# SwiGLU over 8192 rows: four-row groups with all transfers on one DMA queue, in place of two-row tiles with loads and stores on separate queues

## The chip, the cores and the metric

The kernel runs on one core of a Trainium2 chip. The metric is device time in microseconds, the median of the runs. "The span" is the time from the first to the last instruction in one execution that the hardware profiler recorded; all views of the profile are of that execution.

The core has engines that work side by side and wait for each other through semaphores: ScalarE (ACT) applies functions, VectorE (DVE) multiplies, SyncE (SP) and GpSimd (POOL) here only start transfers. A transfer (DMA) between the chip's main memory (HBM) and the on-chip memory (SBUF, 128 partitions) is started by an instruction on SP, ACT or POOL. Each of the three has a queue of its own. The data are moved by 16 DMA engines, which serve all queues.

## The reference

```python
x = np.random.randn(8192, 8192).astype(np.float32)
a, b = np.split(x, 2, axis=-1)
silu_b = b / (1 + np.exp(-b))
return a * silu_b
```

A row of x has 8192 numbers: the first 4096 are a, the last 4096 are b. The output row has 4096. So 268.44 MB are read and 134.22 MB written, and each output needs one function value and one product.

## The kernel before, in words

A tile takes two rows (R = 2) on each of the 128 partitions: 65536 B per partition, 8 MiB, one solid block of x. There are 32 tiles. Three slots in SBUF of that size (`slot0` to `slot2`) are used in turn; together they take 192 KiB of each partition. For each tile:

- `load` (L54, the DMA at L55) is a DMA on SP's queue: x to the slot.
- `swiglu` (L67): ACT applies Silu to b in place (L72), then DVE multiplies a and b and writes the product into the first half of the same slot (L76). The product needs half the room: 32768 B per partition.
- `store` (L81, the DMA at L85) writes that half to the output, 4 MiB. It is issued from ACT's queue; five stores in the middle of the kernel are issued from POOL's, and the stores of the last two tiles from SP's.

Between them the waits are: the gate waits for the load, the product for the gate, the store for the product, and the load of tile i + 3 for the store of tile i, which empties its slot. The order on each engine is written out by hand in the loop at L93, with `manual_schedule`; `declare_no_dep` takes out the waits that follow from others. On SP, the loads stand in the order of the tiles; a load that waits holds back all behind it.

The beginning and the end are cut finer. Tiles 0 to 2 are computed row by row (128x4096). The store of tile 0 is in three pieces (4096, 12288 and 16384 B per partition), and its slot is refilled by two half loads, the second half (32768 B of each 65536 B) as soon as the second row's product is done. The last tile (31) is loaded in two halves and stored in three pieces, the last products being 128x2048.

Of the kernel before, what the change touches and what calls it, by code (L numbers as in the profile page):

```python
# [1 line left out]

# [4 lines left out]

_SILU = mybir.ActivationFunctionType.Silu


@with_exitstack
def kernel(
    ctx: ExitStack,
    tc: tile.TileContext,
    x: bass.AP,
    out: bass.AP,
):

    nc = tc.nc
    N, M = x.shape
    half = M // 2
    P = nc.NUM_PARTITIONS
    R = 2
    BUFS = 3  # L30

    xv = x.tensor.reshape([N // R, R * M]).ap()
    ov = out.tensor.reshape([N // R, R * half]).ap()
    ntiles = N // (P * R)
    last = ntiles - 1

    pool = ctx.enter_context(tc.tile_pool(name="sbuf", bufs=1))
    ctx.enter_context(tc.manual_schedule())
    slots = [pool.tile([P, R * M], x.dtype, name=f"slot{s}") for s in range(BUFS)]
    loads, gates, prods, stores = ([[] for _ in range(ntiles)] for _ in range(4))  # L40

    newest = {}

    def follows_from_others(inst, i, current, earlier):


        targets = [t for kind in current for t in kind[i]]
        targets += [t for kind in earlier for j in range(i % BUFS, i, BUFS) for t in kind[j]]
        for t in targets:
            if t is not newest.get(inst.ins.engine):  # L50
                tc.declare_no_dep(inst.ins, t.ins, reason="ordered by the other waits")
        newest[inst.ins.engine] = inst

    def load(i, c0=0, cw=R * M, free=None):  # L54
        inst = nc.sync.dma_start(  # L55
            out=slots[i % BUFS][:, c0 : c0 + cw], in_=xv[i * P : (i + 1) * P, c0 : c0 + cw]
        )
        if free:
            for t in loads[i - BUFS] + gates[i - BUFS] + prods[i - BUFS] + stores[i - BUFS]:
                if t is not free and t is not newest.get(inst.ins.engine):  # L60
                    tc.declare_no_dep(inst.ins, t.ins, reason="ordered by the other waits")
            newest[inst.ins.engine] = inst
        else:
            follows_from_others(inst, i, [], [loads, gates, prods])
        loads[i].append(inst)

    def swiglu(i, k0=0, k1=R, c0=0, cw=half, gated=None):  # L67
        rows = slots[i % BUFS].rearrange("p (k s c) -> p k s c", k=R, s=2)
        a = rows[:, k0:k1, 0, c0 : c0 + cw]
        b = rows[:, k0:k1, 1, c0 : c0 + cw]  # L70
        o = slots[i % BUFS][:, : R * half].rearrange("p (k c) -> p k c", k=R)
        gate = nc.scalar.activation(out=b, in_=b, func=_SILU)  # L72
        follows_from_others(gate, i, [], [loads, gates, prods, stores])
        if gated:
            gated()
        prod = nc.vector.tensor_mul(out=o[:, k0:k1, c0 : c0 + cw], in0=a, in1=b)  # L76
        follows_from_others(prod, i, [loads], [loads, gates, prods, stores])
        gates[i].append(gate)
        prods[i].append(prod)

    def store(i, c0=0, cw=R * half):  # L81
        eng = nc.scalar if i < last - 1 else nc.sync
        if i % 2 and ntiles // 2 <= i < ntiles // 2 + 10:
            eng = nc.gpsimd
        inst = eng.dma_start(  # L85
            out=ov[i * P : (i + 1) * P, c0 : c0 + cw], in_=slots[i % BUFS][:, c0 : c0 + cw]
        )
        follows_from_others(inst, i, [loads, gates], [loads, gates, prods, stores])
        stores[i].append(inst)

    for i in range(BUFS):
        load(i)
    for i in range(last):  # L93
        if i == 0:

            swiglu(i, 0, 1)
            swiglu(i, 1, 2, gated=lambda: [store(0, 0, half // 4), store(0, half // 4, half * 3 // 4)])
            load(BUFS, M, M, free=prods[0][-1])
            store(i, half, half)
        elif i < BUFS:  # L100
            for k in range(R):
                swiglu(i, k, k + 1)
            store(i)
        else:
            swiglu(i)
            if i == last - 1:
                swiglu(last, 0, 1)
            store(i)
        nxt = i + BUFS
        if nxt == BUFS:  # L110
            load(nxt, 0, M)
        elif nxt < last:
            load(nxt)
        elif nxt == last:
            load(last, 0, M)
            load(last, M, M)

    store(last, 0, half)
    for c0 in range(0, half, half // 2):
        swiglu(last, 1, 2, c0, half // 2)  # L120
    store(last, half, half)


# [1 line left out]
_INS = ['x']  # L125
_OUTS = [((8192, 4096), 'float32')]


# [23 lines left out]
```

## Time and profile before

| | |
|---|---|
| median of 3 runs | 935.29 us (934.9 to 935.36) |
| span of the profiled execution | 934.1 us; no other time of that execution is given |
| VectorE busy | 278.9 us, 30% |
| ScalarE busy | 226.8 us, 24% |
| mean rate of the transfers | 431 GB/s |
| gate (ACT), 128x8192 / 128x4096 | 7029 / 3609 ns |
| product (DVE), 128x8192 / 128x4096 | 8693 / 4425 ns |
| load, 8 MiB, from issue to landing | 37.1 us (median of 30) |
| store, 4 MiB, from ACT's queue | 34.7 us (median of 24) |

How to read the profile: in the row of forty slices, each digit is the busy share of one fortieth of the span in tenths, for the DMA row the mean of the 16 engines. A row of the windows gives, for a stretch of time, its length, the busy time and the number of instructions of each engine, the clock, the share of the DMA engines' time that was filled, and the rate. A packet is counted in the window in which it starts, so short windows can show shares above 1. A row of the timeline gives the start, the length and the engine, and in brackets how long the engine had been idle and what ended that.

Under these views lie the single packet records of the trace: for each packet its queue, start, duration and size. Each DMA of 128 partitions is split over 16 engines, 8 packets on each, and each engine ends its share with a write of 4 B to the semaphore.

### The profile page before, as it was taken

What the parts mean: (1) busy time and instruction counts of PE and PEld (TensorE: products, weight loads), DVE (VectorE), ACT (ScalarE), POOL (GpSimd) and SP (SyncE); (2) the same over time, 40 slices, a digit from 0 to 9 for tenths busy, and PEclk for the clock granted to TensorE, in tenths of its full rate; (3) what the DMA queues carried; (4) which work ended last, traced back from release to release, by engine and by line L of the source; (5) the groups of instructions that cost most, each with busy time, mean ns of one, the idle gap of its engine ahead of it and who ended that gap; (6) DMA issues with size and microseconds to landing.
All of it is one profiled execution on the core that took longest, in us unless ns stands there. A gap on an engine that the chain in (4) does not pass through costs nothing.

```text
span 934.1 us, 228 instructions
## 1 busy us (share of the span) xinstructions
DVE 278.9 (30%) x37; ACT 226.8 (24%) x38; POOL 3.0 (0%) x9
## 2 busy tenths in 40 slices
DVE  0333123332133321333312333133331233312342
ACT  0431320233302333113331133311333113331141
POOL 0000000000000000000000000000000000000000
DMA  9999999999999999999999999999999999999998
GB/s 404 418 425 435 429 450 424 446 429 425 448 420 436 427 450 425 425 439 452 432 415 455 413 443 428 431 445 427 431 428 459 415 428 445 429 445 428 428 427 383
DMA packets 9937, 402.67 MB, mean 431 GB/s; under 512 B 1104, under 2 KB 1104, under 8 KB 1232
## 3 DMA queue, kind: packets, MB, share of 16 engines
q1 hardware_dynamic: 5328, 276.83, 68.6%
q10 hardware_dynamic: 3888, 104.86, 26.0%
q0 software_dynamic: 720, 20.97, 5.2%
q14 instruction: 1, 0.01, 0.0%
HBM read 268.44 MB, written 134.22 MB: 431 GB/s over the span
## 4 chain that ended last, share of the span: by engine, by line
DMA 74%; DVE 10%; ACT 7%; issue 6%; another core or an unknown queue 1%; DVEq 0%; SPq 0%; POOL 0%; ACTq 0%; POOLq 0%
DMA slot<-in_x_dram 40%; DMA out_dram<-slot 34%; DVE slot L76 10%; ACT slot L72 7%; DVEq L147 0%; SPq L55 0%; POOL out_dram L85 0%; ACTq L85 0%; DVEq L76 0%; POOLq L147 0%
## 5 line engine op out<-in xcount | busy, mean ns | idle before, releaser
L76 DVE TENSOR_TENSOR slot<-slot 128x8192 f32<-128x8192 f32 (+2 forms) x37 | 278.9, 7539 | 641.4 <-ACT slot L72 641.1
L72 ACT ACTIVATE slot<-slot 128x8192 f32<-128x8192 f32 (+2 forms) x37 | 225.5, 6105 | 690.0 <-DMA slot<-in_x_dram 690.0
L85 POOL DMA_DIRECT2D out_dram<-slot x5 | 2.8, 558 | 756.8 <-DVE slot L76 756.8
L72 ACT ACT_TABLE_LOAD x1 | 1.3, 1283 | 0.7 <-PEq L136 0.7
L136 POOL MEMSET const-bfloat16-1.0<- 128x1 bf16 x1 | 0.1, 102 | 0.0
L136 POOL MEMSET const-float32-0.0<- 128x1 f32 x1 | 0.1, 98 | 0.2 <-issue 0.2
L136 POOL MEMSET const-float32-1.0<- 128x1 f32 x1 | 0.1, 98 | 0.0
L136 POOL MEMSET const-uint8-127<- 128x1 uint8 x1 | 0.1, 98 | 0.0
## 6 DMA issues: line engine op xcount, KB each, us to landing
out_dram<-slot ACTq DMA_DIRECT2D x24, 4096.0 KB, 34.7
out_dram<-slot POOLq DMA_DIRECT2D x5, 4096.0 KB, 33.8
slot<-in_x_dram SPq DMA_DIRECT2D x4, 4096.0 KB, 29.7
out_dram<-slot SPq DMA_DIRECT2D x1, 4096.0 KB, 19.3
out_dram<-slot SPq DMA_DIRECT2D x2, 2048.0 KB, 14.5
out_dram<-slot ACTq DMA_DIRECT2D x1, 2048.0 KB, 47.0
out_dram<-slot ACTq DMA_DIRECT2D x1, 1536.0 KB, 41.8
out_dram<-slot ACTq DMA_DIRECT2D x1, 512.0 KB, 24.6
```

Source lines behind the costliest of these rows:

```text
L72: gate = nc.scalar.activation(out=b, in_=b, func=_SILU)
L76: prod = nc.vector.tensor_mul(out=o[:, k0:k1, c0 : c0 + cw], in0=a, in1=b)
L85: inst = eng.dma_start(out=ov[i * P : (i + 1) * P, c0 : c0 + cw], in_=slots[i % BUFS][:, c0 : c0 + cw])
L136: nc = _bacc.Bacc("TRN2", target_bir_lowering=False, num_devices=1)
```

## The change

The kernel is written anew around groups of four rows per partition (R = 4, 16 groups). The two first rows of a group (the first pair) and the two last (the second pair) are loaded by a DMA each, 65536 B per partition out of a stride of 131072 B. The products of all four rows go into the first pair's slot, which they fill: 65536 B. One store writes them, 8 MiB.

So a group has a slot that it keeps (`keep`, with the first pair, then the products) and one that the second pair passes through (`thru`). The passing slot is free once the second pair's products are made; the kept one when the store has landed. The first pair of group g + 1 goes into the passing slot of group g, and the second pair into the slot that the store of group g - 1 emptied.

All loads and stores are on SP's queue, in the order: first load of g + 1 (waits for the last product of g), second load of g + 1 (waits for the store of g - 1), store of g (needs the same last product). There are 32 loads and 16 stores. At the beginning three loads are issued, then the fourth after the first group's products. ACT and POOL issue no DMA. The first pair is computed in one step (128x8192), the second pair row by row (128x4096).

```diff
-    R = 2
-    BUFS = 3
+    R = 4
+    ngroups = N // (P * R)
...
+    keep, thru = [0, 2], [1, 1]
+    for g in range(2, ngroups):
+        keep.append(thru[g - 1])
+        thru.append(keep[g - 2])
...
+    def load(g, second):
+        s = (thru if second else keep)[g]
+        inst = nc.sync.dma_start(
+            out=slots[s], in_=xv[g * P : (g + 1) * P, second * 2 * M : (second + 1) * 2 * M]
+        )
+        behind(inst, [s], *([free[s]] if s in free else []))
+        landed[g, second] = inst
+
+    def swiglu(g, second, k0, k1):
+        s, o = (thru if second else keep)[g], keep[g]
+        rows = slots[s].rearrange("p (k s c) -> p k s c", k=2, s=2)
+        a, b = rows[:, k0:k1, 0], rows[:, k0:k1, 1]
+        to = slots[o].rearrange("p (k c) -> p k c", k=R)[:, 2 * second + k0 : 2 * second + k1]
+        gate = nc.scalar.activation(out=b, in_=b, func=_SILU)
+        behind(gate, [s], landed[g, second])
+        prod = nc.vector.tensor_mul(out=to, in0=a, in1=b)
+        behind(prod, {s, o}, gate, *([last[g]] if g in last else []))
+        last[g] = prod
+        free[s] = prod
+
+    def store(g):
+        s = keep[g]
+        inst = nc.sync.dma_start(out=ov[g * P : (g + 1) * P], in_=slots[s])
+        behind(inst, [s], last[g])
+        free[s] = inst
+
+    load(0, 0)
+    load(0, 1)
+    load(1, 0)
+    for g in range(ngroups):
+        swiglu(g, 0, 0, 2)
+        for k in range(2):
+            swiglu(g, 1, k, k + 1)
+        if g == 0:
+            load(1, 1)
+            store(0)
+        elif g + 1 < ngroups:
+            load(g + 1, 0)
+            load(g + 1, 1)
+            store(g)
         else:
-            swiglu(i)
-            if i == last - 1:
-                swiglu(last, 0, 1)
-            store(i)
...
+            store(g)
```

`behind` (new) takes out the waits on earlier users of a slot, except those that are named in the call.

More of the change, by code (lines that the diff above doesn't have):

```diff
@@ L28 @@
     P = nc.NUM_PARTITIONS
-    R = 2
-    BUFS = 3
+    R = 4
+    ngroups = N // (P * R)
     xv = x.tensor.reshape([N // R, R * M]).ap()
     ov = out.tensor.reshape([N // R, R * half]).ap()
-    ntiles = N // (P * R)
-    last = ntiles - 1
     pool = ctx.enter_context(tc.tile_pool(name="sbuf", bufs=1))
     ctx.enter_context(tc.manual_schedule())
-    slots = [pool.tile([P, R * M], x.dtype, name=f"slot{s}") for s in range(BUFS)]
-    loads, gates, prods, stores = ([[] for _ in range(ntiles)] for _ in range(4))
+    slots = [pool.tile([P, 2 * M], x.dtype, name=f"slot{s}") for s in range(3)]
@@ L42, with behind @@
+    touched = [[] for _ in slots]
     newest = {}
[L44 to L51, printed above, removed]
-        newest[inst.ins.engine] = inst
-    def load(i, c0=0, cw=R * M, free=None):
+    def behind(inst, of, *targets):
+        for s in of:
+            for t in touched[s]:
+                if t not in targets and t is not newest.get(inst.ins.engine):
+                    tc.declare_no_dep(inst.ins, t.ins, reason="ordered by the other waits")
+        for s in of:
+            touched[s].append(inst)
+        newest[inst.ins.engine] = inst
+        return inst
@@ L55, in load @@
+    keep, thru = [0, 2], [1, 1]
+    for g in range(2, ngroups):
+        keep.append(thru[g - 1])
+        thru.append(keep[g - 2])
+    free = {}
+    landed = {}
+    last = {}
+    def load(g, second):
+        s = (thru if second else keep)[g]
         inst = nc.sync.dma_start(
-            out=slots[i % BUFS][:, c0 : c0 + cw], in_=xv[i * P : (i + 1) * P, c0 : c0 + cw]
+            out=slots[s], in_=xv[g * P : (g + 1) * P, second * 2 * M : (second + 1) * 2 * M]
         )
[L58 to L62, printed above, removed]
-        else:
-            follows_from_others(inst, i, [], [loads, gates, prods])
@@ L65, in load @@
[L65 to L102, printed above, removed]
-            store(i)
-        else:
-            swiglu(i)
-            if i == last - 1:
-                swiglu(last, 0, 1)
[L108 to L121, printed above, removed]
+        behind(inst, [s], *([free[s]] if s in free else []))
[11 more added lines that the diff above has]
+        free[s] = prod
```

## The prediction

> **What bounds the kernel now.** I read the forty slices and the queue totals first, because a kernel that does two short operations on each byte should be bound by its transfers.
>
> ```profile
> DMA  9999999999999999999999999999999999999998
> GB/s 404 418 425 435 429 450 424 446 429 425 448 420 436 427 450 425 425 439 452 432 415 455 413 443 428 431 445 427 431 428 459 415 428 445 429 445 428 428 427 383
> DMA packets 9937, 402.67 MB, mean 431 GB/s; under 512 B 1104, under 2 KB 1104, under 8 KB 1232
> ...
> q1 hardware_dynamic: 5328, 276.83, 68.6%
> q10 hardware_dynamic: 3888, 104.86, 26.0%
> q0 software_dynamic: 720, 20.97, 5.2%
> ```
>
> The three queues (SP's, ACT's, POOL's) fill 68.6 + 26.0 + 5.2 = 99.8% of 16 engines' span. Both computing engines are idle most of the time (VectorE busy 30%, ScalarE 24%). So the end is set by the sum of packet times, and only three things can change it: what a packet costs, an idle DMA engine, and the two ends of the span. The second view is the windows table:
>
> ```profile
> core 0: us, DVE busy (x) ACT busy (x) POOL busy (x), PEclk, DMA share, GB/s
> ...
> 25.00:54.00 29.00, 16.46 (x4) 12.03 (x4) 0.00 (x0) 1.00 0.96 416
> 54.00:66.00 12.00, 1.24 (x1) 0.00 (x0) 0.00 (x0) 1.00 0.98 397
> ...
> 249.00:510.00 261.00, 78.23 (x9) 63.26 (x9) 0.00 (x0) 1.00 1.00 434
> ...
> 913.00:931.00 18.00, 4.49 (x2) 3.71 (x2) 0.00 (x0) 1.00 1.00 429
> 931.00:932.00 1.00, 0.00 (x0) 0.00 (x0) 0.00 (x0) 1.00 0.39 164
> 932.00:934.10 2.10, 0.00 (x0) 0.00 (x0) 0.00 (x0) 1.00 0.02 8
> ```
>
> The reader should see a steady state with nothing left (share 1.00, 434 GB/s from 249 to 510), a beginning that is a little short of it, and about 2.5 us at the end in which the engines run dry. 402.65 MB at 434 GB/s is 927.8 us, so of the span of 934.1 us no more than about 6 us is not plain transfer. That is the most a new order can win. The Trainium skill ("DMA: Bandwidth & Descriptors", Where 436 GB/s comes from) puts the ceiling at 435.2 GB/s; by it the transfers alone would take 925.2 us, an estimate from that page, which the steady 434 GB/s all but reaches.
>
> The third view is the single packet records. Per engine they are: 240 packets of 65536 B, 272 of 32768 B, 24 of 16384 B, 8 of 12288 B, 8 of 4096 B and 69 semaphore writes of 4 B. Back to back they start 2.414, 1.209, 0.607, 0.456, 0.155 and 0.006 us after each other, whichever direction they go: 65536 B costs 0.004 us less than two times 32768 B. The sum is 579.4 + 328.9 + 14.6 + 3.6 + 1.2 + 0.4 = 928.1 us. What surrounds it: first packets start at 1.74 to 2.73 us and end on average at 5.08, as if the stream began at 5.08 - 2.41 = 2.67. Between 25 and 66 us some load packets take longer than their usual 2.418 us (at 60.5 us all 16 engines have one of 2.9 to 3.4), 0.82 us per engine in all. So the mean engine should end at 2.67 + 928.1 + 0.82 = 931.6; the records show 931.4 to 932.0 for fifteen of them and 932.87 for the last. Then come 0.35 us until the last store has landed (933.21) and 0.9 us of closing. That accounts for 934.1. The median of the timed runs, 935.29, is 1.2 us above the span; I keep that difference.
>
> **The change part by part.**
>
> *Packet sizes.* A load keeps 128 rows of 65536 B, a store now has them too. Per engine: 48 transfers x 8 = 384 packets and 48 semaphore writes. 384 x 2.414 + 48 x 0.006 = 927.3 us, against 928.1: **-0.8 us** (to -0.95 with three decimals more in the spacing). The small first stores (4096, 12288, 16384 B) go with it. That a store of 65536 B moves like a load of that size is read across from 32768 B, where 256 first half-load packets and thousands of store packets all take 1213 ns. Bounds: if it stays in packets of 32768 B, nothing is won.
>
> *One queue in place of three.* ACT's 27 and POOL's 5 store issues go (338 ns and 531 ns each, on engines that wait anyway: worth nothing), and SP issues 48 DMAs of 0.33 us, 16 us in all, beside a span of waiting: nothing. What counts is whether a queue alone keeps 16 engines full where one DMA ends and the next begins. Load after load: SP's queue alone is active until ACT's first store at 30.9 us, and its packets run on across the end of the first load, still 2.414 us apart. Store after store: from 78 to 86 us ACT's queue runs alone, across the end of a store, at 0.607 and then 1.209 us, no gap. Load then store on SP's queue: from 904 us SP issues its last loads and three stores behind them, and the window from 913 to 931 has share 1.00. A load behind a store on the same queue is not in the trace. Bounds: 0, as in the other three turns, and the stretch of the 60.5 us packets, 0.5 us. I take 0, three turns against one odd spot.
>
> *The new wait for the products.* A load into the second pair's slot now waits for that pair's last product instead of a store. Queued behind it on SP are the group's second load and the store, and they wait with it. The cover is the store of the group before, already on the queue: 8 packets x 2.414 = 19.3 us on every engine. The chain under it is in these rows:
>
> ```profile
> 42.64 7.12 ACT L72 ACTIVATE slot<-slot 128x4096 f32<-128x4096 f32 x2 [12.74 <-DMA slot<-in_x_dram]
> 46.29 8.95 DVE L76 TENSOR_TENSOR slot<-slot 128x4096 f32<-128x4096 f32 x2 [10.90 <-ACT slot L72]
> 55.28 0.34 ACTq L85 DMA_DIRECT2D out_dram<-slot  x1
> ```
>
> This is the same pair of rows in single steps: landed 42.64, products done and the next DMA issued at 55.28, 12.6 us later. From SP's first issue (0.74) to the packets it starts took 1.0 to 2.0 us. So the next load is at the engines 14.6 us after the landing at the latest. The landing itself is seen 0.35 us after the last packet, so the slowest engine has 19.3 - 0.35 = 19.0 us of work left then, and one that runs 1.1 us ahead has 17.9. **3.3 us are left over**; cost nothing. If that cover were gone, each missing microsecond would count 15 times. The first pair's gate and product (7.03 + 8.69 = 15.7 us) lie beside the second load (19.3 us) and are done before it lands.
>
> *The wait for the store.* The second load of the next group waits until the previous store has landed: about 0.4 us after its last packet, plus 2.0 for the issue. By then the first load, 19.3 us, runs: 17 us over. Nothing.
>
> *Beginning and end.* The three first loads fill 3 x 19.3 = 58 us, until about 60.6. The fourth is issued 12.6 us after the second landed: 42 + 12.6 = 54.7, at the engines by 56.7. At the end, the last products (12.6 us after the last load) lie under the second to last store (19.3 us), and the last store follows with no gap. The closing 0.35 + 0.9 us stays. The 0.82 us of stretched packets stood beside the first, small, interleaved stores, which go: I take **-0.8 us**, with 0 as the other bound. The straggler was 1.1 us behind the mean engine, half of it by one 0.3 us gap and one packet 0.24 us too long near 675 us; starts alone differ by 0.4. I take 0.8 (from 0.4 to 1.3).
>
> *The loads' stride.* A load now takes 65536 B out of each 131072 B instead of one solid block. Nearest rows: the half loads of tiles 3 and 31 take 32768 B out of each 65536 B, at the usual 1213 ns. I take 0. The other bound is the mild stretch of loads at 31 to 34 us, 2.441 against 2.418: 256 x 0.023 = 5.9 us. The Trainium skill speaks against this part: "DMA: Bandwidth & Descriptors", Latency and other measured facts, gives copies with a row pitch of 512 KiB 207 GB/s per direction against 214 at a padded pitch. Were 128 KiB as bad, the 256 load packets per engine, 618 us, would cost 3.4% or 21 us more, an estimate from that page that no row here shows. The skill's "Perfetto Trace Analysis" (DMA Optimizations) also advises to give loads and stores different issuing engines; with the trace's queue-alone stretches at full rate, it would be worth nothing here.
>
> **Sum.** 2.67 + 927.3 + 0.8 (straggler) + 1.25 (landing and closing) = 932.0 us of span, plus 1.2: **933.2 us**, 0.22% under 935.29.
>
> **The rivals.** A measurement of this kernel can tell about 0.2% from no change, that is 933.4 below and 937.2 above.
>
> 1. *The gain is given back* (0.37). The stretched packets come again (+0.8), or the store packets save nothing (+0.8), or the straggler is at its upper bound (+0.5). 934.0 with one of them, 934.8 with two. For it: the stretches are not explained by anything in the profile. Against: they stand in one place only, where the small stores are.
> 2. *A load behind a store leaves a gap on the one queue* (0.07 with the stride's cost, which looks the same from outside). There are 14 such turns, at 0.5 us each 7.2 us: 940.4, slower. It decides from (937.2 - 933.2) / 14 = 0.28 us per turn. For it: no row shows that turn. Against: the other three turns cost nothing.
> 3. *The products' wait outlasts its cover* (0.04). The chain must grow from 14.6 to above 17.9 us; at 1 us too much the price is 15 us: 948. Against: both engines' durations repeat to within 0.1%.
>
> **Chances and range.** Forecast 0.52, from 932.3 (straggler 0.4, last decimals of the spacing, 0.3 less of first latency) to 933.6 or so. Rival 1 0.37, rivals 2 and 3 0.11. Of forecast and rival 1 together nearly all lies between 932.3 and 935.2; the slower cases are left out. Faster by over 0.2%: 0.51; within: 0.38; slower: 0.11.
>
> **What would show it.** Right: 48 x 128 packets of 65536 B on one hardware queue; share 1.00 in all windows from 66 to 930; SP's wait for the product ending about 13 us after each second landing, with the store still running; from issue to landing about 26 us for a first load, 38 for a second, 57 for a store (19.3 us for itself and for each transfer ahead of it); span near 932. Wrong: windows with share under 1.00 every 58 us, at a load's start (rival 2: short, at each store's end; rival 3: before each first load), or load packets above 2.42 us throughout (the stride).

## The result: 0.4% slower, and the profile after

The changed kernel takes **938.94 us** (median of 4 runs, 938.36 to 940.42) against 935.23 us before (934.9 to 935.36): ratio 1.004, 95% interval 1.0028 to 1.0053. The forecast was 933.2, the range ended at 935.2, and the sign is the other one. The profiled execution has a span of 936.2 us and a time of 938.36; the four spans are 936.2, 936.7, 936.9 and 938.2. Before, in the runs that were made beside the experiments, spans of 933.1 to 934.8 went with times of 934.91 to 936.53.

The page of the changed kernel: slices, packets, queues, and the DMAs' median times from issue to landing.

```profile
DMA  9999999999999999999999999999999999999997
GB/s 403 448 428 423 423 428 448 431 420 448 426 426 445 428 426 437 440 423 437 440 420 440 440 426 431 442 428 423 448 442 414 442 442 417 440 440 412 448 437 344
DMA packets 6914, 402.67 MB, mean 430 GB/s; under 512 B 768, under 2 KB 768, under 8 KB 768
...
q1 hardware_dynamic: 6912, 402.66, 99.6%
...
slot<-in_x_dram SPq DMA_DIRECT2D x32, 32.8
out_dram<-slot SPq DMA_DIRECT2D x16, 57.7
```

One queue carries everything, in 6912 packets: 6144 of data and 768 semaphore writes, as forecast. Busy share and landing times are as forecast too (57 us for a store). Nothing in these lines looks wrong, and that is the first lesson: **a packet that takes longer than it should counts as busy.** The windows show a little more:

```profile
core 0: us, DVE busy (x) ACT busy (x) POOL busy (x), PEclk, DMA share, GB/s
25.00:66.00 41.00, 17.45 (x3) 16.45 (x4) 0.00 (x0) 1.00 1.00 435
66.00:90.00 24.00, 13.62 (x3) 9.39 (x3) 0.00 (x0) 1.00 0.95 393
90.00:249.00 159.00, 43.81 (x8) 35.33 (x7) 0.00 (x0) 1.00 1.01 435
249.00:510.00 261.00, 82.19 (x15) 63.73 (x14) 0.00 (x0) 1.00 1.00 433
510.00:600.00 90.00, 23.63 (x4) 21.18 (x4) 0.00 (x0) 1.00 1.00 431
...
930.00:931.00 1.00, 0.00 (x0) 0.00 (x0) 0.00 (x0) 1.00 0.15 66
931.00:932.00 1.00, 0.00 (x0) 0.00 (x0) 0.00 (x0) 1.00 0.91 393
932.00:933.00 1.00, 0.00 (x0) 0.00 (x0) 0.00 (x0) 1.00 0.15 66
933.00:934.00 1.00, 0.00 (x0) 0.00 (x0) 0.00 (x0) 1.00 0.00 0
```

Two of the same windows of the kernel before:

```profile
66.00:90.00 24.00, 8.85 (x2) 7.12 (x2) 0.00 (x0) 1.00 1.01 434
510.00:600.00 90.00, 26.08 (x3) 22.68 (x4) 1.20 (x2) 1.00 0.99 427
```

From 25 to 66, loads alone, 435 GB/s. From 66 to 90, where the first store follows a load, 393, where it was 434. After that the windows hardly differ: 433 from 249 to 510 where it was 434, and 431 from 510 to 600 where it was 427. They are coarse, too: a packet counts where it starts, so 16 packets of 65536 B (1 MB) on the other side of a border are 44 GB/s in a window of 24 us. The last packets start before 933, yet the span ends at 936.2: some engines are late. A DMA's last packets end at different times on the 16 engines. I call the time between the first and the last of the 16 semaphore writes of one DMA the **spread**. The packet records give it, and the **stretch**: the time by which packets are longer than usual (2418 ns for 65536 B), summed and divided by the 16 engines. A group of stretched packets at one place I call a burst:

```
changed kernel                          at us       stretch per engine   longest
first packets                           1.7             0.75 us            990 ns
last packets of the 4th DMA, a load    77.2             0.92             1321
last packets of the loads ahead of
  the 2nd, 3rd, 4th ... store         136, 194, 252    0.09, 0.15, 0.22   307, 470, 596
all after 95 us                                         1.96
spread at 100, 293, 428, 583 us: 0.50, 1.47, 2.42, 2.99; at the last store 3.55
kernel before: after 95 us 0.03; spread at the last store 1.44
```

Most stretched packets sit in one place: **the last load packet ahead of a store**. It holds 1.68 of the 1.96 us after 95 us. The last packets of a load with a load behind it, and of a store with a load behind it, show less than 0.01 us in sum. Over the 12 turns after 100 us whose last load packets show more than 0.3 us in all 16 engines together, the 8 engines that come first lose 48 ns each, the 8 that come last 232 ns. So the late engines get later, and the spread grows. The last semaphore write of the mean engine comes at 932.86, that of the last at 935.01; before, these were 931.76 and 932.86.

The waits behave as forecast. The changed kernel's timeline around one turn:

```profile
139.63 7.12 ACT L72 ACTIVATE slot<-slot 128x4096 f32<-128x4096 f32 x2 [12.32 <-DMA slot<-in_x_dram]
143.28 8.76 DVE L74 TENSOR_TENSOR slot<-slot 128x4096 f32<-128x4096 f32 x2 [7.24 <-ACT slot L72]
152.06 7.55 SPq L61 DMA_DIRECT2D slot<-in_x_dram  x2
159.66 0.42 SPq L81 DMA_DIRECT2D out_dram<-slot  x1
```

The second pair lands at 139.63, and the next load is issued at 152.06, 12.4 us later, while the store ahead of it still has 7 us to go. The records show no engine idle between DMAs, but for three gaps of 0.2 to 0.3 us on single engines. Two of them go with instruction fetches of 8192 B on queue 14; the trace before has such a fetch at 678.8 us, where the prediction saw a gap.

### The profile page after: what moved, and what is told of

Its sections match the earlier page's. It is cut to its first block, busy times and chain, and to the rows that moved or that the text cites. A ratio compares the mean times of both kernels' runs of the same rounds, so it can differ in the third digit from the quotient of the medians.

```text
span 936.2 us, 235 instructions
## 1 busy us (share of the span) xinstructions
DVE 279.2 (30%) x48; ACT 227.7 (24%) x49; POOL 0.2 (0%) x4
## 3 DMA queue, kind: packets, MB, share of 16 engines
q1 hardware_dynamic: 6912, 402.66, 99.6%
## 4 chain that ended last, share of the span: by engine, by line
DMA 67%; DVE 14%; another core or an unknown queue 9%; ACT 6%; SPq 1%; DVEq 0%; issue 0%
DMA slot<-in_x_dram 62%; DVE slot L74 14%; ACT slot L72 6%; DMA out_dram<-slot 5%; SPq L61 1%; DVEq L126 0%
## 5 line engine op out<-in xcount | busy, mean ns | idle before, releaser
L74 DVE TENSOR_TENSOR slot<-slot 128x4096 f32<-128x4096 f32 (+1 forms) x48 | 279.2, 5845 | 629.9 <-ACT slot L72 629.9
L72 ACT ACTIVATE slot<-slot 128x4096 f32<-128x4096 f32 (+1 forms) x48 | 226.4, 4748 | 675.5 <-DMA slot<-in_x_dram 675.5
```

Source lines behind the costliest of these rows:

```text
L74: prod = nc.vector.tensor_mul(out=to, in0=a, in1=b)
```

## The experiments

Theory 1: a store behind a load on one queue costs time at the turn, and more so (1a) because the engines turn at the same moment and disturb each other. Rivals: the new sizes and strides (theory 2), the computing engines (3), new parts of the output (4), a fixed price of each engine's own turn (1b). Stretch is per engine, over all of a run after 95 us unless said otherwise. Stretch and spread are those of one profiled execution per kernel.

### Stores on their own queue

```diff
-        inst = nc.sync.dma_start(out=ov[g * P : (g + 1) * P], in_=slots[s])
+        inst = nc.scalar.dma_start(out=ov[g * P : (g + 1) * P], in_=slots[s])
```

> The changed kernel with one edit: the stores are issued from ACT's queue, the loads stay on SP's. Theory 1 (a store that follows a load on the same queue stretches the load's last packets: 0.92 us per engine at 77 us, then 0.02 to 0.26 at the turns, until the engines are 3.55 us apart): the bursts of long load packets ahead of each store go, the engines stay within 1.2 us of each other, span 932 to 933.5, 2.5 to 4 us under the changed kernel. Theory 2 (the cause is where the groups read and write: the stride of the loads or the 65536 B stores): the bursts stay, span 935.5 to 937. The time outside the span was 2.2 us for the changed kernel; if that belongs to the one queue it falls to 1.2, if to the absence of POOL's DMAs it stays.

Measured: **1309.5 us**, ratio 1.4001 (1.3982 to 1.402), which neither theory expected. The queues' shares of 16 engines' span, and the windows of one group in this kernel:

```profile
q1 hardware_dynamic: 4608, 268.44, 53.5%
q10 hardware_dynamic: 2304, 134.22, 25.4%
...
197.00:212.00 15.00, 0.12 (x1) 0.00 (x0) 0.00 (x0) 1.00 0.97 350
212.00:250.00 38.00, 0.00 (x0) 1.43 (x1) 0.00 (x0) 1.00 0.98 369
250.00:269.00 19.00, 8.69 (x1) 5.95 (x2) 0.00 (x0) 1.00 0.72 310
269.00:282.00 13.00, 8.76 (x2) 6.77 (x2) 0.00 (x0) 1.00 0.00 0
```

From 269 to 282 nothing moves: gate and product of the second pair, 12.5 us, lie open. On one queue the previous store stood *behind* that pair's load and covered them. On a queue of its own it runs *beside* the loads and is over when they are. From 197 to 250 there is a second cost: 350 to 369 GB/s with engines busy. After 95 us 43% of the load packets are some 0.8 us too long, and 55% of the store packets some 0.3 us, all of 65536 B; 101 us of stretch per engine in all. So this run says nothing on the turn, but what the one queue is for: in this grouping it is not a simplification, it is the cover. The Trainium skill ("DMA: Bandwidth & Descriptors", Rules for kernel authors) says that spreading DMAs over issuing engines doesn't help bandwidth, as all share 16 engines; the measurement goes further, the queue also sets the order. The shares add up to 78.9% of 1307.5 us, against 99.6% of 936.2 on one queue: of the 371 us by which the span grew, some 272 are idle engines and some 99 the longer packets.

### Sizes and strides

Store in two DMAs of 32768 B per partition (e2), two-row tiles as before but on one queue (e3), groups of two solid blocks (e4):

```diff
# e2
-        inst = nc.sync.dma_start(out=ov[g * P : (g + 1) * P], in_=slots[s])
+        for c in (0, M):
+            inst = nc.sync.dma_start(
+                out=ov[g * P : (g + 1) * P, c : c + M], in_=slots[s][:, c : c + M]
+            )
...
# e4 (x as rows of two, out too)
...
-            out=slots[s], in_=xv[g * P : (g + 1) * P, second * 2 * M : (second + 1) * 2 * M]
+            out=slots[s], in_=xv[(2 * g + second) * P : (2 * g + second + 1) * P]
...
```

> The changed kernel with each store cut into two DMAs of 32768 B per partition, still on SP's queue behind the loads. Theory 1 (turn from load to store on one queue): there are as many turns, so the bursts stay at the last load packet, span 936 to 938 (0.8 us more for the packets of half the size). Theory 2a (store packets of 65536 B): the bursts go, span 933 to 934.

> The two-row tiles of the kernel before (solid loads, stores of 32768 B), but all on SP's queue in the order store of i, load of i + 2; rows computed singly; last load in two halves. There are 30 turns from load to store in place of 15. Theory 1: a burst at each turn, so twice as many, and engines 4 to 7 us apart at the end: span 938 to 942. Theory 2 (stride or store size of the groups): no bursts after the first, span 933 to 935.

> The changed kernel with a group made of two solid blocks: each load is one contiguous 8 MiB, and the one store writes two runs of 32768 B per partition. One queue, the same order and waits. Theory 1: the bursts stay, span 936 to 938. Theory 2b (the stride of 131072 B of the loads): the bursts go, span 933 to 934. With e2: if both lose the bursts, the store packets' size is the cause; if this one alone, the stride.

| | time, us | ratio to before | stretch after 95 us | spread |
|---|---|---|---|---|
| changed kernel | 938.94 | 1.004 (1.0028 to 1.0053) | 1.96 us | 3.55 us |
| e2, half stores | 939.32 | 1.0037 (1.0023 to 1.0051) | 3.17 | 3.81 |
| e3, two-row tiles | 939.3 | 1.0047 (1.0034 to 1.006) | 1.31 | 4.72 |
| e4, solid loads | 939.43 | 1.0045 (1.0033 to 1.0058) | 3.43 | 3.26 |

All three keep the bursts at the turns and the drift. Theory 2 falls in both forms. e3 is the cleanest case: the tiles, sizes and strides of the kernel before, yet slower than it; what is left of the difference is the queue, with the order that goes with it and a plainer start and end. (Its spread in the table is that of the last store but one. For the last store, which needs the last products, the engines waited 3.0 us in the mean; the two latest did not wait, so the end, 936.3 us, is theirs.) But e3 also refutes part of theory 1: it has twice as many turns and *less* stretch. Its spread stood at 3.01 at 245 us, 4.24 at 390, 4.71 from 593 on, and from there on the bursts all but stop. So a turn has no fixed price. The 21 us that the prediction estimated from the skill's figures for a row pitch of 512 KiB do not appear at 128 KiB: the solid loads of e4 are no faster (939.43 against 938.94 us).

### Little compute, and always the same output rows

```diff
# e5: 64 of 4096 columns
-        a, b = rows[:, k0:k1, 0], rows[:, k0:k1, 1]
+        a, b = rows[:, k0:k1, 0, :64], rows[:, k0:k1, 1, :64]
...
# e6
...
-        inst = nc.sync.dma_start(out=ov[g * P : (g + 1) * P], in_=slots[s])
+        inst = nc.sync.dma_start(out=ov[0:P], in_=slots[s])
```

> The changed kernel with gates and products on 64 of the 4096 columns of each row (the other columns are stored as they are); all DMAs, waits and their order stay. Theory 1 (the turn from load to store on one queue stretches the last load packets): the bursts stay, 2.5 to 4.5 us of stretch per engine after the first packets, span 935.5 to 938. Theory 3 (the bursts come from the computing engines' work on SBUF or from late issues): the bursts go, span 932 to 933.

> The changed kernel with every store going to the output rows of the first group (the other output rows are not written). Theory 1: no change, bursts at every turn, span 935.5 to 938. Theory 4 (a store that touches a new part of the output pays once for it, ahead of its first packet): the burst at the first store stays, those after it go, span 932.5 to 933.5.

Measured: e5 938.74 us, ratio 1.0038 (1.0024 to 1.0053), 1.29 us of stretch after 95 us and 0.92 before, spread 3.27; e6 939.86 us, 1.0051 (1.0034 to 1.0068), 1.78 and 0.96 us, spread 3.05 at the last but one store (its last store goes to the rows of the one ahead and waited for it, 3.1 us on the mean engine, and the spread closed in that wait; by estimate this costs e6 some 1.3 us more). The bursts stay in both. VectorE is busy 279 us in one and 10 in the other: compute does not make them. Theory 4 falls as well, for all but the one burst at the first store.

### Engines set apart

Six small loads go behind the first load, on fewer and fewer partitions (e7), or each on 16 (e9, the control):

```diff
...
     load(0, 0)
+    for j, n in enumerate((14, 12, 9, 7, 5, 2)):   # e9: six times 16
+        c = slice(j * 2728, j * 2728 + 2728)
+        inst = nc.sync.dma_start(out=slots[2][0:n, c], in_=xv[0:n, c])
...
     load(0, 1)
```

> The changed kernel with six small extra loads behind the first load, on 14, 12, 9, 7, 5 and 2 partitions and so on as many DMA engines, 10912 B each, about 0.4 us a packet: they set the engines apart by up to 2.4 us in steps, at a price of 2.4 us on the last engine. In the changed kernel engines are 0.55 us apart at first, the bursts hit the late ones most, and they fade once the engines are 3 us apart. Theory 1a (engines disturb each other when they turn at the same time): stretch after 66 us falls from 2.9 us per engine to below 1.8, span 936 to 937 in spite of the 2.4 us. Theory 1b (each engine pays for its own turn): stretch stays near 2.9 us, span 938 to 940.

> The control to the staggered kernel: the same six small extra loads at the same place, but each on 16 partitions, so that every engine gets all six and none is set apart. Theory 1a (engines disturb each other when they turn at the same time): the burst at the first turn is back with 0.8 to 1.0 us per engine, and the later ones with 1 to 3 us. If it was the extra loads as such that took the bursts away, they stay away (below 0.5 us after 66 us).

```
                    spread, us, at about                stretch     time
                  100    300    600    last store     after 95 us
changed kernel    0.50   1.47   2.74     3.55            1.96       938.94
e7, set apart     3.27   3.31   3.22     3.86            0.66       943.66
e9, all alike     0.59   1.00   3.05     3.23            1.54       947.49
```

e7 is what theory 1a expects of the stretch: engines 3.3 us apart from the start stay so (3.0 to 3.3 up to 840 us), and counting packets over 30 ns too long only, the bursts are 0.30 us against 1.86. In e9, which has as many small loads, on more partitions, but no setting apart, the engines start 0.5 us apart and drift to 3.2 just as in the changed kernel (1.24 us of such bursts). So **it is the simultaneous turn that costs**: the four traces of these loads and stores without setting apart show 1.09 to 1.86 us of such bursts (e5, e9, e6, the changed kernel), the two with it 0.30 and 0.45 (e7, and e10 below). The drift fades as the engines get further apart, but no sharp distance ends it: in the changed kernel a burst at 835 us still took the spread from 2.9 to 3.6, and in e3 it went on to 4.7. The times don't show the gain (e7's span is 941.8 where 936 to 937 was expected), since the small loads are dear: 268 GB/s from 19 to 33 us in e7, 225 in e9, against 449 in the changed kernel. One expectation failed: the burst at the first store did not come back in e9.

### Engines set apart without extra bytes

> The changed kernel with engines set apart without extra bytes: the first load is cut by partitions, so that 16 of its rows are dealt unevenly (0 to 6 pieces of 10912 B per engine, 1.2 us over the mean at most). Theory 1a: bursts after 66 us below 1 us per engine; the span is then 927.3 + 2.67 + 1.2 + 0.5 + 1.25 = 933 plus what the small pieces cost at the start (in the staggered kernel some 3 us of stretch stood beside them): 933 to 936. Theory 1b: as the changed kernel, 936 to 938.

The first load is cut into 112 partitions and pieces of the other 16:

```diff
-    load(0, 0)
+    parts = [(112, 128, 8184, 16384), (0, 112, 0, 16384)]
+    for j, n in enumerate((14, 11, 9)):
+        c0, c1 = j * 2728, (j + 1) * 2728
+        parts += [(112, 112 + n, c0, c1), (112 + n, 128, c0, c1)]
...
```

Measured: 959.19 us, ratio 1.0252 (1.0238 to 1.0266). The bursts behave as theory 1a expects (0.45 us of packets over 30 ns too long; spread 2.91 at 61 us, 3.72 at 602, 4.2 at most), but the span is 956.0 where 933 to 936 was expected: packets that start before 66 us are 17 us too long on the mean engine. The slices of this kernel's page:

```profile
GB/s 236 225 439 436 436 433 425 433 436 430 436 439 439 430 433 430 433 433 433 436 436 439 430 433 433 433 430 433 434 436 436 436 433 428 433 436 433 430 436 335
```

The first two slices run at 236 and 225 GB/s: packets of the load on 112 partitions took 4.7 us in the median, in place of 2.4.

### Smaller packets at the turn

Loads in two halves of 32768 B (e8), and stores too (e12):

```diff
-        inst = nc.sync.dma_start(
-            out=slots[s], in_=xv[g * P : (g + 1) * P, second * 2 * M : (second + 1) * 2 * M]
-        )
...
+        for k in range(2):
+            c = (2 * second + k) * M
+            inst = nc.sync.dma_start(
+                out=slots[s][:, k * M : (k + 1) * M], in_=xv[g * P : (g + 1) * P, c : c + M]
+            )
...
```

> The changed kernel with each load cut into two DMAs of one row, 32768 B per partition. The packet ahead of the store is then half as long; the packets cost 0.5 us more in all. If the stretch grows with the packet ahead of the turn (the engine's reads of that packet compete with what other engines begin to store): stretch after 66 us is halved, to 1.2 to 1.8 us, span 935 to 936.5. If it is a price of the turn itself: stays near 2.9 us, span 936.5 to 938.5. At the end of e3, where the last load had packets of 32768 B, the burst was 25 ns.

> The changed kernel with every load and every store cut into two DMAs of 32768 B per partition, one queue. The ideal packet sum is 1.6 us longer (768 x 1.2095 + 96 x 0.006 = 929.4). If the drift comes from engines meeting at the turns and grows with the packet ahead, the engines end 1.5 to 2.5 us apart and the span is 935.5 to 937, as with half loads alone; if the drift depends on the stores' packets too, under 1.5 us apart and 934.5 to 935.5.

Measured: e8 938.72 us, 1.0038 (1.0023 to 1.0053), spread 1.02 at 304 us and 2.45 at the end. Bursts of over 30 ns fall to 0.58 us, but 1.3 us come in crumbs of 1 to 29 ns (mostly 5 and 8) on the smaller packets, so stretch is 1.87 us (2.77 after 66 us), not halved. e12: 939.86 us, 1.0046 (1.0034 to 1.0059), spread 0.82 at 304, 1.54 at 604, but 3.13 at the end, stretch 2.19. Smaller packets slow the drift and don't stop it; e12's spread at the end and its span, 938.1, lie above both expectations.

### The kernel before without POOL's stores

```diff
-        if i % 2 and ntiles // 2 <= i < ntiles // 2 + 10:
-            eng = nc.gpsimd
```

> The kernel before with its five stores from POOL issued from ACT like the others. In the kernel before the engines, at 16 loads in a row exactly 1.44 us apart at their ends, are 2.5 us apart from the load that lands at 540 us on, where the first store from POOL began at 526, and that load landed 1.1 us late. If POOL's issue is the cause, that step goes and the time falls by up to 1 us, to 934.3 to 935.0; if something else is, 935.0 to 935.6. Two queues in turn: no burst after 66 us in either case.

Measured: 935.47 us against 935.32, ratio 1.0003 (0.9994 to 1.0012): no difference. The step at 540 us is gone (from 160 to 885 us the spread is 1.78 for each load, 2.93 for each store), but it had not set the end: before, too, the spread is 1.44 again in the last 30 us. After 95 us this kernel has 0.02 us of stretch. Two queues that alternate loads of 65536 B with stores of 32768 B have no common turn, and no drift. No version tried here is faster than the kernel before.

## Why the prediction was wrong, by its steps

- **Turn from load to store: the step that failed.** It was taken at nothing, because the window from 913 to 931 of the profile before has share 1.00. That share cannot show a stretched packet, and the window begins too late: the load's semaphore writes, and with them the turn, stand at 912.0 to 913.5. It is a single turn, behind load packets of 32768 B, of which none is over 23 ns too long. In the changed kernel there are 15 such turns, behind packets of 65536 B: the first cost the mean engine 0.92 us, the 14 after it 1.68 in sum. (With the few stretched packets elsewhere the stretch is 0.96 up to 95 us, without the first packets, and 1.96 after.) The bound that the prediction kept for an unseen turn, 0.5 us, was set against the wrong one: a load behind a store shows next to nothing (none on the store's last packets, at most 0.02 us per engine on the load's first).
- **The straggler: mis-sized, for the same reason.** Taken as 0.8 us over the mean engine, it was 2.15 (935.01 - 932.86). The prediction took it from chance delays; it is fed at the turns, where the late engines lose most.
- **The stretched packets at the start** were to go with the small stores (-0.8). They came back as one burst at the first store (the 0.92 us named above), much as rival 1 said.
- **Packet sum** (-0.8), **beginning, waits and cover**: as forecast. Start to mean end is 2.67 + 927.3 + 2.9 = 932.9, and 932.86 was measured. The chain took 12.4 to 12.5 us of 19.3. Rival 3 did not occur.
- **The stride:** nothing (e4).
- **Span to time:** taken as 1.2 us from a span and a median of different executions. Runs with both show 1.7 to 1.8 for before, and 2.1 to 2.2 for the changed kernel.

Two slips in it had no effect on the sum: SP issued its last loads at 879.5 us at the latest, and from 904 us the stores only; and 14 turns at 0.5 us are 7.0 us, not 7.2.

The account, against the forecast of 933.2: 0.9 (first turn) + 2.0 (stretch after it, mostly at the turns) + 1.35 (straggler) make the profiled span 936.2 in place of 932.0. The median run lies 0.6 above that execution, and the time outside the span adds 0.95. Sum 5.8, measured 5.7.

Rival 2 had the nearest mechanism, a price on the one queue where direction turns, and its chance of 0.07 was far too small; it put the price on the wrong turn and took it as constant.

What stays open: why engines that turn together stretch the last load packet, which no record shows; why the first store brings a burst of 0.6 to 1.3 us in most kernels with the change, but none in e7, e9 and e10; and whether the burst of 0.55 us at 60.5 us in the kernel before is of the same kind, as its first store packet started at 34.4.

## What to carry to other kernels

When transfers fill the span, look at the durations of single packets and at how far the DMA engines are apart, not at busy shares: a share of 1.00 is compatible with losing time. Here loads of 65536 B and stores of 32768 B that alternated on two queues let the 16 engines go on without drift (0.02 to 0.03 us of stretch), where long blocks in turn on one queue let them drift by 3 us; with stores of 65536 B on two queues, in e1, there was 101 us of stretch. Before moving stores to another queue, ask which waits they cover in their present place; here it was 12 us per group.

## What the runs showed of the hardware

- Engines that turn from load to store together on one queue drift apart, to 3 to 4.7 us (0.50 to 3.55 in the changed kernel, 0.6 to 4.7 in e3); set 3.3 us apart at the start, they stayed there up to 840 us and ended 3.9 apart (e7).
- Of the load packets of 65536 B beside store packets of 65536 B on two queues, 43% took some 0.8 us more (350 to 369 GB/s in e1); beside store packets of 32768 B, nothing (434 GB/s before).
- A load on 112 partitions ran at about half rate (236 GB/s), and small loads on 16 partitions or fewer brought the rate to 225 to 268 for 14 us. The Trainium skill ("SBUF — State Buffer", Door 1) says that the rate depends on how many of 16 ports the partitions reach. By its table the first 16 partitions reach 4 of them, but the first 112 reach all 16, so it does not explain the slow load on 112; no run here shows the cause of either.
- The time outside the span was 1.74 to 1.79 us in e1, e2, e3, e7 to e10 (medians) and 2.1 to 2.2 in the changed kernel, e4, e5 and e6. The latter four have an instruction fetch of 8192 B that starts 1.9 us after the last instruction. That is a coincidence seen, not a cause tried.
